# A two-layer float32 trunk on one core: norm weights and roots moved as whole rows, the first transfers and transposes re-ordered, the last residual added into the PSUM banks

## The chip, the core and the metric

The kernel runs on one core of one Trainium2 chip. TensorE (PE) multiplies matrices into the banks of PSUM; VectorE (DVE) and ScalarE (ACT) do the elementwise work between SBUF and PSUM; SyncE (SP), and ScalarE where the code says so, issue transfers (DMA). Each engine runs its own instructions in program order, and they wait for each other by semaphores. The metric is the device time of one execution in microseconds (us), lower is better.

## The reference

A causal decoder trunk on `x` of 1 x 1024 x 1024 float32, two layers. Each layer is a token mixer and a squared-ReLU MLP, each with an RMSNorm ahead and a residual add behind; a last RMSNorm gives the output.

```python
def reference(x, norm_mix_w, norm_mlp_w, final_norm_w, attn_w_in, ...):
    for i in range(2):
        h = rmsnorm(x, norm_mix_w[i])
        if i == 0: x = x + dilated_attention(h, attn_w_in[0], attn_w_out[0])
        else:      x = x + gla_mixer(h, gla_w_in[0], ...)
        h = rmsnorm(x, norm_mlp_w[i])
        a = relu(h @ mlp_w_up[i]);  x = x + (a * a) @ mlp_w_down[i]
    return rmsnorm(x, final_norm_w)
```

`rmsnorm(x, w)` is `x * rsqrt(mean(x*x) + 1e-5) * w` over the 1024 features. `dilated_attention` projects to queries, keys and values of three head groups, each with its own window and dilation; `gla_mixer` is gated linear attention in chunks of 64. The MLP is 1024 to 4096 to 1024.

## The kernel before, in words

All work is written out in program order, by hand, for every engine; there is no scheduler. A float32 product is made of three products of rounded parts: each operand is cut into a high part (`...h`, rounded by ScalarE) and a low part (`...l`, the rest, subtracted by VectorE), and high x high, high x low and low x high are summed in PSUM. On top of that the large products use a form with seven half-size products in place of eight, so that also sums of blocks (`s1` to `s4`) are cut.

**The start.** The first product is the values projection (`vals`), made from the raw `x`, with the norm's weights multiplied in as `x` is turned, and the norm's root (one number for each token) multiplied in as results leave PSUM. A constant tile `warm` is multiplied three times at L1533, for which nothing waits. Meanwhile SP issues the transfers in this order: the columns from 512 on of the first 128 tokens of `x`, the identity, the same columns of the next 128 tokens, the norm weights (`wcol`, one column of 128 weights per block of 128 features, read element by element at L1542), the first two weight blocks `raw` of 512 KB, the other columns of `x`, two more blocks `kept`, then the rest of `x`. A semaphore pool of eight serves SP's transfers in rotation.

`first_turn` (L334) transposes 256 tokens x 512 features of `x` through PSUM in eight 128 x 128 pieces, in two banks of four. `first_high` (L340, ScalarE) rounds each bank times `wcol` into `a12h` (later `a11h`). `first_low` (L346 and L348, VectorE) writes the unrounded float32 copy `a` from the bank and then subtracts. `rounded` (L1038, ScalarE) and `remain` (L1044, VectorE) cut a weight block into `dh` and `dl`. Then `product(n, blocks)` (L1060) multiplies: products 0 and 1 with `a12`, 2 and 3 with `a11`, each first for the token blocks [0, 1], then for [2, 3]; product 4 is the first with a sum (`s1`). With its third argument it takes the parts in the order high-high, high-low, low-high for all blocks, so that the low weights are wanted last.

`turn(p)` (transposes L318, copies by ScalarE L321) does the same for the next 256 tokens each; `cut` rounds (ScalarE L356) and subtracts (VectorE L358) the halves; `squares` sums the squares of `x` (ScalarE L1570, VectorE L1567); `roots(half)` makes the roots (`rstd_of`, L213 to L222) and stores them column-wise, element by element, to `rscr` in DRAM (L1575), from where the attention reads them as a row far later (L1678). `total`, `sums` and `sum1` to `sum4` make sums of blocks and of results on VectorE and ScalarE (L1014, L1142, L1146, L362). From step 8 on a loop takes one product after the other.

**The end.** The last MLP's down projection (`Down`) keeps the two halves of the result in PSUM (`pA`, `pB`) and the running residual in `xs`. Its steps 0 to 55 are again products of 24 matmuls. After step 53 the last two, 54 and 55, run for one block of 128 tokens at a time, and as each block is done, `add` puts the bank `pB` and the residual together into `xs` (VectorE, L1928), `half_out` sums its squares (ScalarE, L2006; the other half was done before), `root` and `small` make the norm's factor (L2027 to L2035), and `upper` (ScalarE, L2040) and `lower` (VectorE, L2045) scale the two halves and store them. One block's factor is finished while the next block multiplies.

Of the kernel before, what the change touches and what calls it, by code (L numbers as in the profile page):

```python
# [41 lines left out]
def hybrid_trunk(ctx, tc, x, norm_mix, norm_mlp, norm_fin, a_in, a_out, g_in, g_up, g_b, g_nw,  # L42
# [16 lines left out]
    def t2(shape, dt, name):  # L59
        return wk.tile(shape, dt, name=name, tag="t2", bufs=8)  # L60
# [4 lines left out]
    def sm(shape, name):  # L65
        return wk.tile(shape, F32, name=name, tag="sm", bufs=19)
# [215 lines left out]
    class Halves:  # L282
# [40 lines left out]
        def first_turn(self, c):  # L323

            name = ("a11", "a12")[c]
            self.a[0, c] = self.one("a", F32)
            self.up.h[name] = Split(self.one(name + "h", F32R), self.one(name + "l", F32R))
            self.ps = getattr(self, "ps", {})
            for kp in range(2):
                ps = self.ps[c, kp] = bank("pT").rearrange("p (k t) -> p k t", k=2)  # L330
                for k in range(2):
                    for i in range(2):
                        col = 512 * c + 256 * kp + 128 * k
                        pe.transpose(ps[:, k, 128 * i:128 * i + 128], self.xn[0][i][:, col:col + 128], ident)  # L334
# [7 lines left out]
        def first_low(self, c, kp):  # L342
            ps, s, a = self.ps.pop((c, kp)), self.up.h[("a11", "a12")[c]], self.a[0, c]
            for k in range(2):
                n = 2 * kp + k
                dve.tensor_scalar(a[0][:, n, :256], ps[:, k, :], self.wcol[:, 4 * c + n:4 * c + n + 1], None, op0=OP.mult)  # L346
            sl = slice(2 * kp, 2 * kp + 2)
            dve.tensor_tensor(s.lo[0][:, sl, :256], a[0][:, sl, :256], s.hi[0][:, sl, :256].bitcast(F32), op=OP.subtract)  # L348
# [1183 lines left out]
    for n in range(3):  # L1532
        pe.matmul(ps, warm[:, :128], warm, start=True, stop=True)  # L1533
    wcol = sm([P, KT], "wcol")
    x0 = [[k4([P, D], F32, "x0") for _ in range(2)] for _ in range(NB // 2)]

    def load_x0(p, i, sl=slice(0, D)):
        sp.dma_start(x0[p][i][:, sl], x[0, 256 * p + 128 * i:256 * p + 128 * i + 128, sl])
    load_x0(0, 0, slice(512, D))
    sp.dma_start(ident, ident_d)  # L1540
    load_x0(0, 1, slice(512, D))
    sp.dma_start(wcol, norm_mix[0].rearrange("(k p) -> p k", p=P))  # L1542
    vals.load(0)
# [13 lines left out]
    hs.wcol = wcol  # L1557
# [14 lines left out]
    def roots(half):  # L1572

        y = vals.roots[half] = rstd_of(sums[half], 4, 1.0 / D)
        sp.dma_start(rscr[512 * half:512 * half + 512].rearrange("(t p) -> p t", p=P), y)  # L1575

    hs.first_turn(1)
    hs.first_high(1, 0)
    hs.first_low(1, 0)
    vals.rounded(0)  # L1580
    hs.first_high(1, 1)
    vals.remain(0)
    hs.first_low(1, 1)
    vals.rounded(1)
# [9 lines left out]
    vals.rounded(3)  # L1594
    vals.remain(3)
# [11 lines left out]
    vals.product(0, [2, 3])  # L1607
    vals.sums(2)
    vals.product(1, [2, 3])
    vals.sums(4)  # L1610
    squares(1)
    hs.turn(2)
    hs.sum1(0)
    hs.cut("s1", 0)
    vals.product(2, [2, 3])
    vals.total(4)
    hs.turn(3)
    vals.sums(3)
    vals.rounded(4)
# [45 lines left out]
    for n in range(8, vals.STEPS):  # L1665
        if n == 9:
            for c in range(2):
                hs.cut("a22", c)
        if n >= 10:
            ahead.step()  # L1670
# [176 lines left out]
    class Down:  # L1847
# [153 lines left out]
        def half_out(self, t, n):  # L2001
            ss, o = self.fin[t]
            sl = slice(512 * n, 512 * n + 512)
            r = self.rows(4 + t)[:, sl]
# [6 lines left out]
        def run_end(self):  # L2011
# [31 lines left out]
            def lower(t, y):  # L2043
                o = self.fin.pop(t)[1][:, :512]
                dve.scalar_tensor_tensor(o, self.rows(4 + t)[:, :512], y, self.wbc[:, :512], op0=OP.mult, op1=OP.mult)  # L2045
                sp.dma_start(out[0, 512 + 128 * t:640 + 128 * t, :512], o)

            for t in range(4):
# [5 lines left out]
                self.add("B", 1, t, 0)  # L2054
# [506 lines left out]
```

## Time and profile before

| | us |
|---|---|
| median of 3 runs (lowest, highest) | 2576.76 (2575.3, 2578.85) |
| profiled execution, its own time | 2576.74 |
| its span | 2574.6 |
| PE busy | 2560.6 |
| DVE busy | 1865.7 |
| ACT busy | 1281.0 |

The granted TensorE clock of the profiled execution is 0.999. In the rows of the profile, `128x512 f32` is partitions x elements and type of what is written, `x4` a number of like instructions shown as one row, and `[1.46 <-ACT dh L1038]` the idle time of the engine ahead of the instruction and what ended it. PEld is TensorE's loading of the stationary operand, SPq and ACTq are issues of transfers. Matmuls are pipelined: a duration of 0.39 stands for one matmul by itself, the pace is the distance of the starts.

### The profile page before, as it was taken

Reading aid. Unit: us, or ns where it says so; the run is one execution under the profiler, and the core shown is the slowest. Engines: PE = TensorE matmul, PEld = TensorE weight load, DVE = VectorE, ACT = ScalarE, POOL = GpSimd, SP = SyncE. Lnnn points to the kernel's source line nnn. Section 1 sums busy time; section 2 is a strip of 40 time slices with the busy share of each in tenths; the row PEclk is TensorE's granted clock in tenths of the full one; section 3 lists DMA queues with packets and bytes.
Section 4 is the critical chain, followed back from the end, with each engine's and each line's share of the span. In section 5 each row is a group of like instructions: output and inputs, shape, how many; then the busy total and the mean of one; then the engine's idle time right before and its main releaser. Section 6 shows DMA issues by size and latency. Waiting matters only on the chain.

```text
span 2574.6 us, 34634 instructions
## 1 busy us (share of the span) xinstructions
PE 2560.6 (99%) x12582; PEld 2119.2 (82%) x12582; DVE 1865.7 (72%) x2990; ACT 1281.0 (50%) x2326; POOL 20.2 (1%) x24
## 2 busy tenths in 40 slices
PE   9999999999999999999999999999999999999998
PEld 7888888888888888888888888888888888888887
DVE  7766888888888766788668795787666666566666
ACT  6443445555555445666534453554335555453344
POOL 0000000000000000000000000110000000000000
PEclk9999999999999999999999999999999999999999
DMA  6886465656566747799788865777545644495543
GB/s 170 269 274 199 107 162 142 161 148 153 153 156 175 240 172 253 267 334 338 267 322 290 280 220 196 262 248 283 174 162 199 236 158 139 147 348 199 187 148 128
DMA packets 359196, 544.86 MB, mean 212 GB/s; under 512 B 26640, under 2 KB 182672, under 8 KB 359024
## 3 DMA queue, kind: packets, MB, share of 16 engines
q1 hardware_dynamic: 358880, 542.38, 64.8%
q8 instruction: 99, 1.62, 0.3%
q14 instruction: 73, 0.60, 0.1%
q10 hardware_dynamic: 144, 0.26, 0.0%
HBM read 339.45 MB, written 177.93 MB: 201 GB/s over the span
## 4 chain that ended last, share of the span: by engine, by line
PE 67%; DVE 2%; DMA 1%; ACT 1%; issue 1%; SPq 0%; DVEq 0%; ACTq 0%
PE pB L1922 14%; PE pX L848 11%; PE pA L1922 10%; PE pV L848 8%; PE pY L848 4%; PE pZ L848 4%; PE pB L1060 3%; PE pA L1060 3%; PE pd L196 2%; PE pd L198 2%; PE pd L197 2%; PE pT L259 1%; PE pO L2384 1%; PE pO L2382 0%; PE pU L2365 0%
## 5 line engine op out<-in xcount | busy, mean ns | idle before, releaser
L1922 PE MATMUL pB<-dh 128*128 128x512 f32 x512 | 199.2, 389 | 0.0
L1922 PE MATMUL pB<-dl,dh 128*128 128x512 f32 x512 | 199.2, 389 | 0.0
L1922 PE MATMUL pB<-dh,dl 128*128 128x512 f32 x512 | 199.2, 389 | 0.0
L205 DVE TENSOR_TENSOR dl<-sin,dh 128x1024 fp32r<-128x1024 f32 x112 | 136.6, 1220 | 61.7 <-ACT dh L202 58.9
L848 PE MATMUL pV<-s4h,wd 128*128 128x512 f32 x480 | 161.5, 398 | 0.4 <-DVE qk L2118 0.4
L202 ACT ACTIVATE dh<-sin 128x1024 fp32r<-128x1024 f32 x112 | 117.8, 1052 | 78.6 <-PE pB L1922 29.9
L1922 PE MATMUL pA<-dh 128*128 128x512 f32 x384 | 149.6, 390 | 0.0
L1922 PE MATMUL pA<-dh,dl 128*128 128x512 f32 x384 | 149.4, 389 | 0.0
L1922 PE MATMUL pA<-dl,dh 128*128 128x512 f32 x384 | 149.4, 389 | 0.0
L853 ACT ACTIVATE e<-pX 128x512 f32<-128x512 f32 x108 | 64.4, 596 | 154.3 <-PE pX L848 154.2
L202 ACT ACTIVATE dh<-kept 128x1024 fp32r<-128x1024 f32 x64 | 67.8, 1060 | 146.4 <-DVE kept L1887 102.0
L786 DVE TENSOR_TENSOR wbl<-t,wbh 128x1024 fp32r<-128x1024 f32 x48 | 58.8, 1226 | 78.8 <-ACT wbh L785 78.8
L1922 PEld LDWEIGHTS pB<-dl,dh 128*128 128x128 f32 x512 | 96.1, 188 | 20.1
L1922 PEld LDWEIGHTS pB<-dh,dl 128*128 128x128 f32 x512 | 96.1, 188 | 19.9
L1922 PEld LDWEIGHTS pB<-dh 128*128 128x128 f32 x512 | 96.1, 188 | 19.9
L848 PEld LDWEIGHTS pV<-s4h,wd 128*128 128x128 f32 x480 | 90.1, 188 | 20.3 <-DVE qk L2118 0.8
L1210 ACT ACTIVATE pt<-pt,orow 128x256 f32<-128x256 f32 (+1 forms) x128 | 59.8, 468 | 92.7 <-DVE orow L1208 89.4
L848 PE MATMUL pX<-s3h,wgh 128*128 128x512 f32 x240 | 96.8, 403 | 0.0
L848 PE MATMUL pX<-s2h,wbh 128*128 128x512 f32 x240 | 95.9, 400 | 0.1
L848 PE MATMUL pV<-s1h,wbh 128*128 128x512 f32 x240 | 95.6, 398 | 0.0
L848 PE MATMUL pY<-a12h,wah 128*128 128x512 f32 x240 | 95.3, 397 | 0.0
L848 PE MATMUL pX<-a11h,wah 128*128 128x512 f32 x240 | 95.0, 396 | 0.0
(369 smaller groups left out, 7232.1 us busy)
## 6 DMA issues: line engine op xcount, KB each, us to landing
sin<-acts SPq DMA_DIRECT2D x112, 512.0 KB, 4.3
acts<-s SPq DMA_DIRECT2D x64, 512.0 KB, 3.5
raw<-in_mlp_w_down_dram SPq DMA_DIRECT2D x64, 512.0 KB, 5.1
raw<-in_attn_w_in_dram SPq DMA_DIRECT2D x96, 256.0 KB, 4.4
cw<-c SPq DMA_DIRECT2D x192, 128.0 KB, 2.3
raw<-in_mlp_w_up_dram SPq DMA_DIRECT2D x48, 512.0 KB, 6.1
acts<-c SPq DMA_DIRECT2D x64, 256.0 KB, 3.3
kept<-in_mlp_w_down_dram SPq DMA_DIRECT2D x32, 512.0 KB, 7.3
```

What stands on the lines that cost most here:

```text
L196: pe.matmul(ps, sh, mh, start=start, stop=False)
L197: pe.matmul(ps, sh, ml, start=False, stop=False)
L198: pe.matmul(ps, sl, mh, start=False, stop=stop)
L202: act.activation(hi, src, AF.Copy)
L205: dve.tensor_tensor(lo, src, hi.bitcast(F32), op=OP.subtract)
L259: pe.transpose(ps[e][:, 64 * n:64 * n + 64], src[k, :], ident[k, k], tile_position=(64 * e, 0))
L786: self.remain(lambda: dve.tensor_tensor(lo, src, hi.bitcast(F32), op=OP.subtract))
L848: pe.matmul(st[b], u[:, k, :], v, start=first and k + n == 0, stop=k == 3 and n == 2, skip_group_check=True)
L853: act.activation(e, self.st[p]["X"], AF.Copy)
L1060: pe.matmul(self.acc[s][t], parts[k][v == 2][:, 128 * t:128 * t + 128], (th, tl)[v == 1][:, k, :], start=fresh and m + k + v == 0, stop=m ...
L1210: act.activation(pt[:, i, :128 * n], pt[:, i, :128 * n], AF.Exp, scale=-1.0, bias=m, accum_out=self.row[:, r, HD:HD + 1])
L1922: pe.matmul(self.acc[s][t], a[:, k, c], b[:, k, :], start=fresh and m + k + v == 0, stop=m == 7 and k == 1 and v == 2, skip_group_check=True)
```

## The change

Line numbers move by 6 at the start and by some 30 at the end. What it does:

- The constant tile is multiplied once with 512 and once with 256 columns (L1539) in place of three times with 512.
- The norm weights come as 8 rows of 128 (`wrow`), are transposed on TensorE (L1592) and copied to `wcol` by ScalarE (L1593).
- The second piece of `x` is issued on ScalarE's queue (L1543) in place of SP's, and the first weight block comes as two loads of 256 KB (L1551). Its rounding is shared: the first half by VectorE (L1597), the second by ScalarE (L1599).
- `first_turn` can do one bank of four transposes at a time, and the first copies stand between the two.
- `first_low` subtracts straight from the bank (one fused operation for each 128 x 256, L347); the float32 copy `a` is made by ScalarE (`first_keep`, L354), eight instructions of 128 x 256.
- `roots` no longer stores; `spread(half)` transposes the roots (L1586), copies the 4 x 128 result (ScalarE, L1588) and stores rows. It stands behind `turn(3)` for the first half and in step 14 for the second.
- Product 0 for the blocks [2, 3] is cut in two, with `turn(2)`'s halves between; `turn(3)` stands ahead of product 2 for [2, 3]; `squares(1)` and the sums around it move with them.
- At the end, four additions of the residual into the four banks `pB` (L2079) stand ahead of products 54 and 55, which go on adding to these banks; `half_out` and `lower` read the bank.

ScalarE's program at the start shows several of these at once. Before (numbers behind the names are buffers; `raw` and `kept` are weight blocks, `pT` a bank of transposes):

```order
L963 ACT_TABLE_LOAD
L340 ACTIVATE a12h_248<-pT_250,wcol_215 128x256 x2
L1038 ACTIVATE dh_265<-raw_228 128x1024
L340 ACTIVATE a12h_248<-pT_255,wcol_215 128x256 x2
L1038 ACTIVATE dh_274<-raw_230 128x1024
L340 ACTIVATE a11h_295<-pT_297,wcol_215 128x256 x2
L1038 ACTIVATE dh_312<-kept_234 128x1024
```

and with the change:

```order
L969 ACT_TABLE_LOAD
L1543 DMA x0_215<-in_x_dram 128x512
L1593 ACTIVATE wcol_247<-pT_248 128x8
L341 ACTIVATE a12h_252<-pT_254,wcol_247 128x256 x2
L1599 ACTIVATE dh_259<-raw_227 128x512
L341 ACTIVATE a12h_252<-pT_264,wcol_247 128x256 x2
L1044 ACTIVATE dh_275<-raw_230 128x1024
L354 ACTIVATE a_251<-pT_254,wcol_247 128x256 x2
L354 ACTIVATE a_251<-pT_264,wcol_247 128x256 x2
L341 ACTIVATE a11h_302<-pT_304,wcol_247 128x256 x2
L1044 ACTIVATE dh_318<-kept_234 128x1024
```

A transfer stands ahead of the first copy, the first rounding is half as long, and the copies at L354 stand between the second block's rounding and the next turned half.

VectorE's program at the end, before, from the last block's add on (`xs` is the residual, `fin` the output rows, `v`, `t`, `y` the root's small numbers):

```order
L1928 TENSOR_TENSOR xs_20421<-pB_21814,xs_20421 128x512
L2045 SCALAR_TENSOR_TENSOR fin_22007<-xs_20421,y_22114,wbc_21452 128x512
L2028 TENSOR_SCALAR v_22141<-ss_22012 128x1
L2033 SCALAR_TENSOR_TENSOR t_22143<-y_22142,v_22141 128x1
L2034 TENSOR_SCALAR t_22143<-t_22143 128x1
```

and with the change, from the adds on, which now stand ahead of the first block's root:

```order
L2079 TENSOR_TENSOR pB_21828<-pB_21828,xs_20364 128x512
L2079 TENSOR_TENSOR pB_21829<-pB_21829,xs_20364 128x512
L2079 TENSOR_TENSOR pB_21830<-pB_21830,xs_20438 128x512
L2079 TENSOR_TENSOR pB_21831<-pB_21831,xs_20438 128x512
L2058 TENSOR_SCALAR v_22077<-ss_21978 128x1
L2063 SCALAR_TENSOR_TENSOR t_22079<-y_22078,v_22077 128x1
```

The adds are no longer between a block's last matmul and its square sum; all four come together.

The diff, cut to its core:

```diff
@@ -320,16 +320,17 @@
                 for k in range(2):
                     act.activation(dst[:, k, :], ps[:, k, :], AF.Copy, scale=self.wcol[:, 2 * kp + k:2 * kp + k + 1])
 
-        def first_turn(self, c):
+        def first_turn(self, c, kps=(0, 1)):
 
             name = ("a11", "a12")[c]
-            self.a[0, c] = self.one("a", F32)
-            self.up.h[name] = Split(self.one(name + "h", F32R), self.one(name + "l", F32R))
+            if kps[0] == 0:
+                self.a[0, c] = self.one("a", F32)
+                self.up.h[name] = Split(self.one(name + "h", F32R), self.one(name + "l", F32R))
             self.ps = getattr(self, "ps", {})
-            for kp in range(2):
+            for kp in kps:
                 ps = self.ps[c, kp] = bank("pT").rearrange("p (k t) -> p k t", k=2)
-                for k in range(2):
-                    for i in range(2):
+                for i in range(2):
+                    for k in range(2):
                         col = 512 * c + 256 * kp + 128 * k
                         pe.transpose(ps[:, k, 128 * i:128 * i + 128], self.xn[0][i][:, col:col + 128], ident)
 
@@ -340,12 +341,17 @@
                 act.activation(s.hi[0][:, n, :256], ps[:, k, :], AF.Copy, scale=self.wcol[:, 4 * c + n:4 * c + n + 1])
 
         def first_low(self, c, kp):
-            ps, s, a = self.ps.pop((c, kp)), self.up.h[("a11", "a12")[c]], self.a[0, c]
+            ps, s = self.ps[c, kp], self.up.h[("a11", "a12")[c]]
             for k in range(2):
                 n = 2 * kp + k
-                dve.tensor_scalar(a[0][:, n, :256], ps[:, k, :], self.wcol[:, 4 * c + n:4 * c + n + 1], None, op0=OP.mult)
-            sl = slice(2 * kp, 2 * kp + 2)
-            dve.tensor_tensor(s.lo[0][:, sl, :256], a[0][:, sl, :256], s.hi[0][:, sl, :256].bitcast(F32), op=OP.subtract)
+                dve.scalar_tensor_tensor(s.lo[0][:, n, :256], ps[:, k, :], self.wcol[:, 4 * c + n:4 * c + n + 1],
+                                         s.hi[0][:, n, :256].bitcast(F32), op0=OP.mult, op1=OP.subtract)
+
+        def first_keep(self, c, kp):
+            ps, a = self.ps.pop((c, kp)), self.a[0, c]
+            for k in range(2):
+                n = 2 * kp + k
+                act.activation(a[0][:, n, :256], ps[:, k, :], AF.Copy, scale=self.wcol[:, 4 * c + n:4 * c + n + 1])
 
         def split(self, name, src, c, hi, lo):
             h = self.up.h
@@ -1529,18 +1535,20 @@
     warm = t2([P, 512], F32, "warm")
     dve.memset(warm, 0.0)
     ps = bank("pw")
-    for n in range(3):
-        pe.matmul(ps, warm[:, :128], warm, start=True, stop=True)
-    wcol = sm([P, KT], "wcol")
+    for n in (512, 256):
+        pe.matmul(ps[:, :n], warm[:, :128], warm[:, :n], start=True, stop=True)
     x0 = [[k4([P, D], F32, "x0") for _ in range(2)] for _ in range(NB // 2)]
 
-    def load_x0(p, i, sl=slice(0, D)):
-        sp.dma_start(x0[p][i][:, sl], x[0, 256 * p + 128 * i:256 * p + 128 * i + 128, sl])
+    def load_x0(p, i, sl=slice(0, D), eng=sp):
+        eng.dma_start(x0[p][i][:, sl], x[0, 256 * p + 128 * i:256 * p + 128 * i + 128, sl])
+    wrow = t2([P, 512], F32, "wrow")
     load_x0(0, 0, slice(512, D))
+    load_x0(0, 1, slice(512, D), act)
     sp.dma_start(ident, ident_d)
-    load_x0(0, 1, slice(512, D))
-    sp.dma_start(wcol, norm_mix[0].rearrange("(k p) -> p k", p=P))
-    vals.load(0)
+    sp.dma_start(wrow[:KT, :P], norm_mix[0].rearrange("(k p) -> k p", p=P))
+    t = vals.raw[0] = k4([P, 2, 512], F32, "raw")
+    for k in range(2):
+        sp.dma_start(t[:, k, :], a_in[512 + 128 * k:640 + 128 * k, vals.first[0]:vals.first[0] + 512])
     vals.load(1)
     for i in range(2):
         load_x0(0, i, slice(0, 512))
@@ -1554,7 +1562,7 @@
         k = slice(64 * e, 64 * e + 64)
         sp.dma_start(masks[k, 256:320], msk[k, 128 + 64 * e:192 + 64 * e])
     hs = Halves(None, None, vals, None)
-    hs.wcol = wcol
+    wcol = hs.wcol = sm([P, KT], "wcol")
     hs.xn = dict(enumerate(x0))
 
     sums = {}
@@ -1572,16 +1580,31 @@
     def roots(half):
 
         y = vals.roots[half] = rstd_of(sums[half], 4, 1.0 / D)
-        sp.dma_start(rscr[512 * half:512 * half + 512].rearrange("(t p) -> p t", p=P), y)
-
-    hs.first_turn(1)
+
+    def spread(half):
+        ps = bank("pT")
+        pe.transpose(ps[:4, :P], vals.roots[half], ident)
+        t = t2([P, 512], F32, "rrow")
+        act.activation(t[:4, :P], ps[:4, :P], AF.Copy)
+        sp.dma_start(rscr[512 * half:512 * half + 512].rearrange("(t p) -> t p", p=P), t[:4, :P])
+
+    ps = bank("pT")
+    pe.transpose(ps[:, :KT], wrow[:KT, :P], ident[:KT, :KT])
+    act.activation(wcol, ps[:, :KT], AF.Copy)
+    hs.first_turn(1, (0,))
+    th = k4([P, 2, 512], F32R, "dh")
+    vals.cut[0] = th, vals.raw.pop(0)
+    dve.tensor_copy(th[:, 0, :], vals.cut[0][1][:, 0, :])
     hs.first_high(1, 0)
+    act.activation(th[:, 1, :], vals.cut[0][1][:, 1, :], AF.Copy)
+    hs.first_turn(1, (1,))
     hs.first_low(1, 0)
-    vals.rounded(0)
+    vals.remain(0)
     hs.first_high(1, 1)
-    vals.remain(0)
+    vals.rounded(1)
+    hs.first_keep(1, 0)
     hs.first_low(1, 1)
-    vals.rounded(1)
+    hs.first_keep(1, 1)
     vals.remain(1)
     vals.product(0, [0, 1], True)
     hs.first_turn(0)
@@ -1592,6 +1615,8 @@
     vals.remain(2)
     hs.first_low(0, 1)
     vals.rounded(3)
+    hs.first_keep(0, 0)
+    hs.first_keep(0, 1)
     vals.remain(3)
     vals.product(1, [0, 1], True)
     vals.product(2, [0, 1], True)
@@ -1604,19 +1629,22 @@
     vals.load(5)
     hs.cut("a11", 1)
     roots(0)
-    vals.product(0, [2, 3])
+    vals.product(0, [2], True)
+    hs.turn(2, (0, 2))
+    vals.product(0, [3], True)
+    hs.turn(2, (1, 3))
     vals.sums(2)
+    hs.sum1(0)
     vals.product(1, [2, 3])
+    hs.cut("s1", 0)
     vals.sums(4)
+    hs.turn(3)
+    spread(0)
+    vals.total(4)
+    vals.rounded(4)
+    vals.sums(3)
     squares(1)
-    hs.turn(2)
-    hs.sum1(0)
-    hs.cut("s1", 0)
     vals.product(2, [2, 3])
-    vals.total(4)
-    hs.turn(3)
-    vals.sums(3)
-    vals.rounded(4)
     vals.total(5)
     vals.remain(4)
     vals.rounded(5)
@@ -1666,6 +1694,8 @@
         if n == 9:
             for c in range(2):
                 hs.cut("a22", c)
+        if n == 14:
+            spread(1)
         if n >= 10:
             ahead.step()
         if n == vals.STEPS - 4:
@@ -2001,7 +2031,7 @@
         def half_out(self, t, n):
             ss, o = self.fin[t]
             sl = slice(512 * n, 512 * n + 512)
-            r = self.rows(4 + t)[:, sl]
+            r = self.rows(4 + t)[:, sl] if n else self.acc["B"][t]
             junk = t2([P, 512], F32, "junk")
             act.activation(junk, r, AF.Square, accum_out=ss[:, n:n + 1])
             if n:
@@ -2042,16 +2072,17 @@
 
             def lower(t, y):
                 o = self.fin.pop(t)[1][:, :512]
-                dve.scalar_tensor_tensor(o, self.rows(4 + t)[:, :512], y, self.wbc[:, :512], op0=OP.mult, op1=OP.mult)
+                dve.scalar_tensor_tensor(o, self.acc["B"][t], y, self.wbc[:, :512], op0=OP.mult, op1=OP.mult)
                 sp.dma_start(out[0, 512 + 128 * t:640 + 128 * t, :512], o)
 
+            for t in range(4):
+                dve.tensor_tensor(self.acc["B"][t], self.acc["B"][t], self.rows(4 + t)[:, :512], op=OP.add)
             for t in range(4):
                 self.product(54, [t])
                 self.product(55, [t])
                 if t:
                     y = small(t - 1)
                     upper(t - 1, y)
-                self.add("B", 1, t, 0)
                 if t:
                     lower(t - 1, y)
                 self.half_out(t, 0)
```

## The prediction

> **What bounds the kernel now.** I read the page first, then the timelines of both ends, the transfers by the moment of their issue, and the middle only where the ends run into it. The page says that the profiled execution is TensorE from end to end:
>
> ```profile
> PE 2560.6 (99%) x12582; PEld 2119.2 (82%) x12582; DVE 1865.7 (72%) x2990; ACT 1281.0 (50%) x2326; POOL 20.2 (1%) x24
> ```
>
> The span is 2574.6, the execution's own time 2576.74, so 2.14 us lie around the span; the median of the runs is 2576.76, the same number. Only 14.0 us of the span have no matmul in them, so an edit at the ends can win a few microseconds at most. 0.2%, about what a measurement of this kernel tells from no change, is 5.15 us.
>
> **The start.** TensorE counts as busy there while it only warms up on zeros, or crawls:
>
> ```profile
> 0.73 1.28 ACT L963 ACT_TABLE_LOAD   x1 [0.73 <-PEq L2550]
> 1.48 5.14 PE L1533 MATMUL pw<-warm 128*128 128x512 f32 x6 [1.48 <-DVE warm L1530]
> 6.46 1.04 PE L334 MATMUL pT<-ident,x 128*128 128x128 f32 x8
> 7.84 1.06 ACT L1038 ACTIVATE dh<-raw 128x1024 fp32r<-128x1024 f32 x1
> 8.95 1.19 PE L1060 MATMUL pB<-dh,a12h 128*128 128x512 f32 x4 [1.46 <-ACT dh L1038]
> 11.82 1.04 PE L334 MATMUL pT<-ident,x 128*128 128x128 f32 x8
> 19.83 1.17 PE L1060 MATMUL pA<-dh,a11h 128*128 128x512 f32 x4
> ```
>
> The columns are start, duration, engine, line, operation. The first transposes stand at 6.46, product 0 from 8.95 to 11.82, product 3 at 19.83. What they wait for are transfers:
>
> ```profile
> 1.65 0.42 SPq L1538 DMA_DIRECT2D x<-in_x_dram  x1
> 2.59 1.57 SPq L1004 DMA_DIRECT2D raw<-in_attn_w_in_dram  x2
> ...
> x<-in_x_dram SPq DMA_DIRECT2D x1, 256.0 KB, 3.5
> wcol<-in_norm_mix_w_dram SPq DMA_DIRECT2D x1, 4.0 KB, 4.0
> raw<-in_attn_w_in_dram SPq DMA_DIRECT2D x1, 512.0 KB, 5.2
> raw<-in_attn_w_in_dram SPq DMA_DIRECT2D x1, 512.0 KB, 6.1
> x<-in_x_dram SPq DMA_DIRECT2D x1, 256.0 KB, 5.8
> ...
> 3.50:4.00 0.50, 0.50 (x2) 0.19 (x1) 0.00 (x0) 0.00 (x0) 0.00 (x0) 1.00 0.96 291
> 4.00:4.50 0.50, 0.50 (x2) 0.29 (x1) 0.00 (x0) 0.00 (x0) 0.00 (x0) 1.00 0.60 61
> 4.50:5.00 0.50, 0.50 (x1) 0.04 (x1) 0.00 (x0) 0.00 (x0) 0.00 (x0) 1.00 0.44 31
> ```
>
> The last number of an issue is microseconds to landing; the last three of a window are granted clock, share of the DMA engines and GB/s. Issued at 1.65, the x half lands at 5.2; the norm weights, issued between it and 2.59, land some 4.0 later, about 6.1; the two weight blocks (2.59, and half of 1.57 later) at 7.8 and 9.5. While the 1024 single elements of the norm weights are in flight the engines move 61 and 31 GB/s instead of 291. The two windows lost (230 + 260) x 0.5 = 245 KB, 0.84 us at 291 GB/s; I take 0.9.
>
> **The middle.** Product 4, the first after the shared start, waits for ScalarE and then VectorE:
>
> ```profile
> 33.71 3.16 ACT L321 ACTIVATE a<-pT,wcol 128x256 f32<-128x256 f32 x8
> 34.60 1.38 PE L318 MATMUL pT<-ident,x 128*128 128x128 f32 x8 [0.49 <-ACT a L321]
> 39.00 1.23 DVE L1044 TENSOR_TENSOR dl<-kept,dh 128x1024 fp32r<-128x1024 f32 x1 [2.31 <-ACT dh L1038]
> 39.02 1.20 PE L1060 MATMUL pB<-dh,s1h 128*128 128x512 f32 x4 [0.28 <-ACT dh L1038]
> 55.98 0.19 PEld L1060 LDWEIGHTS pA<-dl,s2h 128*128 128x128 f32 x1 [0.35 <-DVE dl L1044]
> 40.00:44.00 4.00, 4.00 (x19) 3.29 (x19) 4.00 (x7) 1.24 (x2) 0.00 (x0) 1.00 0.31 112
> ```
>
> From 40 to 44 VectorE has no free time (4.00 of 4.00, the number behind PEld's), and at 55.98 TensorE is held up by it. What the start wins reaches the end of the kernel only as far as VectorE's chain, which begins at 39.00 with `dl`, also comes earlier.
>
> **Step 1, transfers.** With the norm weights as 8 whole rows, the 0.9 us come back. The first weights, now two loads of 256 KB, land at 7.8 - 0.9 = 6.9, the second block at 9.5 - 0.9 = 8.6. The x half on ACT's queue is issued behind the table load, 0.73 + 1.28 = 2.01, instead of at 1.65. Its price there is in no row; bounds are the first load's and those of the loads queued behind the weights (5.8): 0.74 + 2.9 = 3.6 as the earliest landing, 7.8 as the latest. I take the row of the same transfer, 3.5, so 5.5:
>
> ```profile
> 0.74 0.39 SPq L1538 DMA_DIRECT2D x<-in_x_dram  x1
> x<-in_x_dram SPq DMA_DIRECT2D x1, 256.0 KB, 2.9
> ```
>
> What is queued behind the issue on ACT is its first copy, which needs the data anyway. Up to about 5.9 the landing costs nothing, since product 0 then waits for the weights; each us later costs one.
>
> SP's queue has one issue less (the x half) and one more (the weights' second load), about 0.4 us each, so what stands behind them is issued as before.
>
> **Step 2, from the landing to product 0.** Transposes at 5.5, the wcol transpose and its copy ahead of them hidden, a pair of copies (0.84 in the row, 0.74 to ScalarE's next start at 7.84), rounding of the first half by VectorE as the weights land (6.9 plus 0.53, half of the 1.06 of the whole block, to 0.69, the 128x512 row), the second by ScalarE; product 0's `dl` part waits for one subtraction of 1.23 (the `dl` row at 39.00). Before, product 0's twelve matmuls took 8.95 to 11.82, 0.24 each; four of them behind a `dl` ready at about 8.8 then end near 9.8 instead of 11.82. The second block's weights (8.6 + 1.06 + 1.23 = 10.9 for the remainder, needed by product 1's last four) allow product 1 2.0 us earlier too.
>
> ```profile
> 7.10 0.84 ACT L340 ACTIVATE a12h<-pT,wcol 128x256 fp32r<-128x256 f32 x2 [5.08 <-PE pT L334]
> 7.97 0.88 DVE L346 TENSOR_SCALAR a<-pT,wcol 128x256 f32<-128x256 f32 x2 [6.54 <-ACT a12h L340]
> 8.88 0.69 DVE L348 TENSOR_TENSOR a12l<-a,a12h 128x512 fp32r<-128x512 f32 x1
> 15.80 1.07 ACT L1570 ACTIVATE junk<-x 128x1024 bf16<-128x1024 f32 x1
> 20.41 1.06 ACT L356 ACTIVATE a12h<-a 128x1024 fp32r<-128x1024 f32 x1
> 30.17 0.19 PEld L1060 LDWEIGHTS pA<-dh,a11h 128*128 128x128 f32 x1 [0.41 <-ACT a L321]
> ```
>
> **Step 3, work that moves to ScalarE.** VectorE's pair plus subtraction (0.88 + 0.69 per half) becomes two fused operations from PSUM. No row shows that form on 128x256: it lies between 0.35, half of the 128x512 subtraction, and 0.79, a copy of the pair plus half of that subtraction (0.44 + 0.35); I take 0.44, the row that reads the same bank. This frees 4 x 0.69 = 2.8 us of VectorE. In return ScalarE makes the eight f32 copies, 0.40 each by the eight at L321 (3.16), so 3.2 us between 8.6 and 19. ScalarE's work from the second block on, each 0.1 under its row since rows overlap as the pair's does: roundings 3 x 0.96, pairs 2 x 0.74, eight copies 3.2, two squares 2.1, four copies 1.6 and the cut of 0.96 end at 8.6 + 12.2 = 20.8; before, the same cut ends at 21.5. ScalarE has no idle time left in this stretch, and wins only 0.7 us of the 2.0. Where product 0's second half waits for that cut and its VectorE remainder, TensorE loses some 0.8 us, and again 0.7 in product 2, at the copies of its last transposes. The spreading of the transposes between products wins part of it back: the stalls at 30.17 and 34.60 (0.41 and 0.49, and 0.5 of the slow pace behind them) go, 1.4 in all. Done by rows for each engine up to product 4 this comes to 36.75 instead of 39.02: 2.3 us.
>
> **Step 4, into the VectorE stretch.** `dl` of product 4's block stands at about 36.1 in the same working, 2.9 earlier. So VectorE's chain gains more than TensorE's, and of the small stalls behind it (0.35 at 55.98) part goes. I take 2.4 us for the start, bounds 2.3 and 2.9. The moved squares and `total` are the same instructions; the second roots' three loose operations are hidden under 24 matmuls per product.
>
> **Step 5, the roots.** The column-wise store of 512 elements becomes a 4x128 transpose, a small copy and a row store, twice. Its landing frees nothing early: `rscr` is read at 224.7. TensorE pays three small transposes of about 0.1 each, two of them outside the idle start, and ScalarE the two copies: 0.1 us at most stays, taken whole.
>
> **Step 6, the tail.**
>
> ```profile
> 2559.43 0.69 DVE L1928 TENSOR_TENSOR xs<-pB,xs 128x512 f32<-128x512 f32 x1 [8.58 <-PE pB L1922]
> 2567.17 0.39 PE L1922 MATMUL pB<-dh,dl 128*128 128x512 f32 x1
> 2567.59 0.69 DVE L1928 TENSOR_TENSOR xs<-pB,xs 128x512 f32<-128x512 f32 x1
> 2567.61 0.72 ACT L2040 ACTIVATE fin<-fin,y 128x512 f32<-128x512 f32 x1 [0.73 <-PE pB L1922]
> 2568.32 0.63 ACT L2006 ACTIVATE junk<-xs 128x512 f32<-128x512 f32 x1
> ```
>
> The last add (2567.59, 0.69, handoff 0.04) stands between the last matmul and the square at 2568.32. Without it the square starts as the bank is done, 2567.6; the scaling ahead of it on ScalarE (2567.61) comes 0.7 earlier with its own chain. That is -0.7 us. The four adds move into VectorE's 8.58 us of idle time. Each waits for its own bank's last matmul of product 53; the first bank is done 9 matmuls, 2.0 us, before product 54 touches it, so an add of 0.69 has 1.35 us to spare. Were this cover gone, one add would stand in front of product 54 and take the 0.7 back. The square and the last scaling read the bank where they read a row before; ScalarE's copies out of banks above (0.40 for 256) speak for no loss beyond 0.2, which I leave to the range.
>
> **The sum**: 2576.74 - 2.4 - 0.7 + 0.1 = 2573.7.
>
> **Rivals.** (1) All stalls of the start go: the stalls of step 3 after product 0 (0.8 + 0.7) do not come since the copies are shorter than I think, and VectorE's chain follows. Then 2573.7 - 1.5, and another 0.9 for the short waits like that at 55.98, of which this needs two or three: 2571.3. For it: ScalarE's rows are busy spans with overlaps. Against: VectorE's 4.00 of 4.00. Chance 0.15.
>
> (2) The pace of TensorE. Weight loads take 0.34 us while it warms up and 0.14 for the same shape later:
>
> ```profile
> L1533 PEld LDWEIGHTS pw<-warm x6: 288/338/338, 1.5 to 5.1; 128*128 128x128 f32 x6
> L334 PEld LDWEIGHTS pT<-ident,x x16: 139/141/231, 5.9 to 12.5; 128*128 128x128 f32 x16
> ```
>
> The quick pace came 4.4 to 5.0 us after the first matmul. The changed warm-up is half as long and ends near 1.48 + 3 x 0.86 = 4.05 (half of the row's 5.14); then TensorE idles till 5.5. If the pace must be earned anew from there, product 0 runs at up to 0.338/0.141 = 2.4 times its time, which adds some 2 us to its first eight matmuls; half of it hides behind the wait for `dl`, 1.0 stays: 2574.7, 0.13. The granted clock reads 1.00 throughout, so the page's clock row cannot decide it. The Trainium skill (TensorE: Matmul & The Clock Gate, "Part 1: The HAM clock gate") has full clock only after a busy window of about 3.4 us; the trace's durations agree (0.338 before 5.1, 0.141 after 5.9), its clock column does not.
>
> (3) Slower: the x half on ACT's queue lands late, because it is issued after the table load and stands behind the weight loads. From 5.9 each us costs one; the gain of 3.0 is gone, and no more is won, at a landing of about 9.0, which is 7.0 us after the issue. The row of the 512 KB block of x, queued deeper, shows 9.3:
>
> ```profile
> x<-in_x_dram SPq DMA_DIRECT2D x6, 512.0 KB, 9.3
> ```
>
> At 9.3 it lands at 11.3, 5.4 past 5.9: 2573.7 + 5.4 = 2579.1. Against it: only 320 KB, x and the identity, are issued ahead of it. 0.05.
>
> (4) Given back in the VectorE stretch: `dl` comes no earlier than TensorE's own gain of 0.6 there, because the eight copies delay ScalarE's roundings ahead of it: 2576.74 - 0.6 - 0.7 + 0.1 = 2575.5, 0.09.
>
> (5) The x half takes the 5.8 of the x load that is issued among the weight loads, and lands at 7.8: the 1.9 past 5.9 go, for 2575.6. For it, its weight-load neighbours are issued within 1 us; against, the 3.5 and 2.9 of the issues at 1.65 and 0.74, of which the one had two transfers before it. 0.10. The Trainium skill (DMA: Bandwidth & Descriptors, "Issuing engines are not separate DMA queues") speaks for this one: transfers started by different engines run on the same 16 DMA engines and interleave, and another engine saves the issue alone; no row of this trace has two issuing engines at the start.
>
> **How the numbers follow.** Forecast 0.48, rivals in their order 0.15, 0.13, 0.05, 0.09, 0.10. The range takes in rival 1 with 0.7 of scatter below it, 2570.6, and ends 1.1 above rivals 4 and 5, at 2576.7; only rival 3 and the scatter of a median of three runs (2575.3 to 2578.85 before) lie outside, less than 2 in 10. Faster by over 0.2% is below 2571.6, which is most of rival 1 and little of the forecast: 0.15. Slower by over 0.2%, above 2581.9, needs rival 3 at its worst: 0.03. The rest, 0.82, is within 0.2%.
>
> **What would show it.** Transposes near 5.5 and not past 5.9 (step 1); product 0's first matmul near 7.2 and its end near 9.8 (step 2); ScalarE without idle time from 8.5 to 20 (step 3); the first `pB<-dh,s1h` near 36.7 (step 4); the square of the last block 0.0 instead of 0.7 after the last matmul (step 6), and the four adds done before product 54 needs them. A weight load of 0.34 in product 0 would speak for rival 2, transposes past 9 for rival 3, and product 4 early with longer VectorE waits behind it for rival 4.

## The result: slower by 27 us, spread over thousands of matmuls

The changed kernel takes 2604.02 us (median of 5, 2603.41 to 2606.11) against 2576.76 (2575.3 to 2578.85): a ratio of 1.0107, 95% interval 1.0092 to 1.0122. The forecast was 2573.7, with a range up to 2576.7. The profiled execution took 2605.88, its span is 2604.0.

The first lines of the page of the changed kernel:

```profile
span 2604.0 us, 34650 instructions
PE 2592.9 (100%) x12583; PEld 2119.9 (81%) x12583; DVE 1865.7 (72%) x2987; ACT 1283.4 (49%) x2337; POOL 20.3 (1%) x24
```

VectorE and ScalarE do what they did before (1865.7 and 1281.0 there), and TensorE has one instruction more. It is busy 32.3 us longer, and waits for less: 11.1 us of the span are without a matmul, 14.0 before. So the loss is no wait. It must lie in the pace, and a view that shows pace is the one by windows, because it counts. Before, then after; the columns are the window, its length, PE's busy time with the number of matmuls that run in it, granted clock, DMA share and GB/s:

```profile
100.00:200.00 100.00, 100.00 (x443) 1.00 0.83 287
1100.00:1200.00 100.00, 99.88 (x440) 1.00 0.98 334
1300.00:1400.00 100.00, 100.00 (x443) 1.00 0.82 292
2100.00:2200.00 100.00, 100.00 (x443) 1.00 0.45 153
2400.00:2500.00 100.00, 100.00 (x443) 1.00 0.49 158
```

```profile
100.00:200.00 100.00, 100.00 (x431) 1.00 0.79 271
1100.00:1200.00 100.00, 100.00 (x432) 1.00 0.97 334
1300.00:1400.00 100.00, 100.00 (x443) 1.00 0.85 303
2100.00:2200.00 100.00, 100.00 (x432) 1.00 0.45 152
2400.00:2500.00 100.00, 100.00 (x443) 1.00 0.54 174
```

In both kernels TensorE hardly rests in these windows (99.88 of 100 us at the least), and the granted clock is 1.00. In 100 us the kernel before runs 443 matmuls (440 in the window with the short rests); the changed one 431 or 432 in the values projection (100 to 200) and in the MLPs' up projections (1100 and 2100), and again 443 in the down projections (1300 and 2400). The starts themselves say the same more finely. The table has the mean distance of neighbouring starts (those of 215 to 245 ns), worked out from all starts of a line:

| product (line before, after) | matmuls | before, ns | after, ns |
|---|---|---|---|
| values, in the second layer also gates (L1060, L1066) | 1680 | 227.0 | 232.7 |
| up projections (L848, L854) | 5040 | 227.6 | 232.4 |
| down projections (L1922, L1952) | 2688 | 226.7 | 226.7 |

The line of the up projections, L848, also makes the attention's queries and keys (2016 of the 5040) and the keys of the second layer's mixer (336); the MLPs' own 2688 go from 226.8 and 226.7 in the two layers to 232.4 in both. Some 1650 and 4755 of the distances lie in the range: 1650 x 5.7 + 4755 x 4.8 ns = 9.4 + 22.8 = 32.2 us. That is more than the 29.4 us between the two profiled spans, so that the rest of the change must have won some of it back.

What do the slow lines have in common? Not the instructions, which are the same, but the addresses of their operands. The working tiles are cut from pools, one for each size of tile, which are laid out in the order in which they are first used (the addresses are those of the two built programs). Before, the small tiles' pool (19 tiles of 96 bytes per partition, 1824 bytes) is first used by `wcol`, ahead of `x0`, the first tile of the pool of 4 KB tiles. The change creates `wcol` later, behind `x0`, so the 4 KB pool moves down by 1824 bytes and the small pool goes behind it; the pool of 8 KB tiles stays:

| start, bytes in a partition | before | after |
|---|---|---|
| pool of 4 KB tiles (weights) | 21696 | 19872 |
| pool of 8 KB tiles (turned activations) | 124096 | 124096 |
| difference | 102400 = 400 x 256 | 104224 = 407 x 256 + 32 |

Most matmuls of the values and up lines take one operand from each pool; the down projections take both from the 4 KB pool, where nothing moves against each other. That was the theory to test. One group does not fit its simplest form, that each matmul goes by its own two operands: the low parts `s2l`, `s3l` and `s4l` lie in the 4 KB pool too, so the 720 matmuls at L854 and 240 at L1066 that use them have both operands there. They stand between matmuls that use both pools, and they are slower too: 231.0 and 233.4 ns from their start to the next (227.3 and 226.9 before).

### The profile page after: what moved, and what is told of

The parts are those of the page before. It is cut to its first block, busy times and chain, and to the rows that moved or that the text cites. A ratio compares the mean times of both kernels' runs of the same rounds, so it can differ in the third digit from the quotient of the medians.

```text
span 2604.0 us, 34650 instructions
## 1 busy us (share of the span) xinstructions
PE 2592.9 (100%) x12583; PEld 2119.9 (81%) x12583; DVE 1865.7 (72%) x2987; ACT 1283.4 (49%) x2337; POOL 20.3 (1%) x24
## 4 chain that ended last, share of the span: by engine, by line
PE 68%; DVE 2%; ACT 1%; DMA 1%; issue 0%; SPq 0%; DVEq 0%; ACTq 0%
PE pB L1952 13%; PE pX L854 12%; PE pA L1952 10%; PE pV L854 8%; PE pY L854 4%; PE pZ L854 4%; PE pB L1066 3%; PE pA L1066 3%; PE pd L196 2%; PE pd L197 2%; PE pd L198 2%; PE pT L259 1%; PE pO L2415 1%; PE pO L2413 0%; PE pU L2396 0%
## 5 line engine op out<-in xcount | busy, mean ns | idle before, releaser
L1952 PE MATMUL pB<-dl,dh 128*128 128x512 f32 x512 | 199.2, 389 | 0.0
L1952 PE MATMUL pB<-dh,dl 128*128 128x512 f32 x512 | 199.2, 389 | 0.0
L1952 PE MATMUL pB<-dh 128*128 128x512 f32 x512 | 199.2, 389 | 0.0
L854 PE MATMUL pV<-s4h,wd 128*128 128x512 f32 x480 | 163.0, 401 | 0.2 <-DVE qk L2149 0.2
L1952 PE MATMUL pA<-dh 128*128 128x512 f32 x384 | 149.6, 390 | 0.0
L1952 PE MATMUL pA<-dl,dh 128*128 128x512 f32 x384 | 149.4, 389 | 0.0
L1952 PE MATMUL pA<-dh,dl 128*128 128x512 f32 x384 | 149.4, 389 | 0.0
L1952 PEld LDWEIGHTS pB<-dh,dl 128*128 128x128 f32 x512 | 96.1, 188 | 20.1
L1952 PEld LDWEIGHTS pB<-dh 128*128 128x128 f32 x512 | 96.1, 188 | 19.9
L1952 PEld LDWEIGHTS pB<-dl,dh 128*128 128x128 f32 x512 | 96.1, 188 | 19.8
L854 PEld LDWEIGHTS pV<-s4h,wd 128*128 128x128 f32 x480 | 90.2, 188 | 21.5 <-DVE qk L2149 0.6
L854 PE MATMUL pX<-s3h,wgh 128*128 128x512 f32 x240 | 97.5, 406 | 0.0
L854 PE MATMUL pV<-s1h,wbh 128*128 128x512 f32 x240 | 96.7, 403 | 0.0
L854 PE MATMUL pY<-a12h,wah 128*128 128x512 f32 x240 | 96.4, 402 | 0.0
L854 PE MATMUL pX<-s2h,wbh 128*128 128x512 f32 x240 | 96.3, 401 | 0.0
L854 PE MATMUL pX<-a11h,wah 128*128 128x512 f32 x240 | 96.3, 401 | 0.0
```

Source lines behind the costliest of these rows:

```text
L854: pe.matmul(st[b], u[:, k, :], v, start=first and k + n == 0, stop=k == 3 and n == 2, skip_group_check=True)
L1952: pe.matmul(self.acc[s][t], a[:, k, c], b[:, k, :], start=fresh and m + k + v == 0, stop=m == 7 and k == 1 and v == 2, skip_group_check=True)
```

## Time at the two ends

The start of the changed kernel, from its timeline, then its TensorE windows and the first product with a sum:

```profile
0.73 1.28 ACT L969 ACT_TABLE_LOAD   x1 [0.73 <-PEq L2581]
0.76 0.39 ACTq L1543 DMA_DIRECT2D x<-in_x_dram  x1
4.77 1.09 PE L335 MATMUL pT<-ident,x 128*128 128x128 f32 x8
7.39 2.00 PE L1066 MATMUL pB<-dh,a12h 128*128 128x512 f32 x4 [1.53 <-DVE dh L1597]
11.96 1.04 PE L335 MATMUL pT<-ident,x 128*128 128x128 f32 x8
...
6.00:7.00 1.00, 0.00 (x0) 1.00 0.93 340
8.00:9.00 1.00, 1.00 (x3) 0.50 1.01 307
...
L1066 PE MATMUL pB<-dh,s1h x16: 395/396/396, 38.4 to 47.5; 128*128 128x512 f32 x16
```

The transposes stand at 4.77 (6.46 before), product 0 at 7.39 (8.95). But TensorE had nothing to do from 6 to 7 us, and from 7.8 to 11.2 us the granted clock is 0.50: the first four matmuls take 2.00 us instead of 1.19 (part of this is a wait for the second half of the weights; without the half clock they take 1.56, as a run below shows), and the next transposes come at 11.96, later than the 11.82 of before. Product 4 starts at 38.4 instead of 39.02.

The end:

```profile
2584.59 2.74 DVE L2079 TENSOR_TENSOR pB<-pB,xs 128x512 f32<-128x512 f32 x4 [3.81 <-PE pB L1952]
2597.08 0.39 PE L1952 MATMUL pB<-dh,dl 128*128 128x512 f32 x1
2597.51 0.60 ACT L2036 ACTIVATE junk<-pB 128x512 f32<-128x512 f32 x1
2600.18 0.38 ACTq L2071 DMA_DIRECT2D out_dram<-fin  x1
```

From the last matmul's start to its block's square it is 0.43 us (1.15 before), to the last issue 3.10 (3.86 before). The four adds are done at 2587.3 and no matmul waits for them.

## Experiments: is it the place of the tiles?

**Addresses of before, all else changed.**

```diff
+    wcol = sm([P, KT], "wcol")
     x0 = [[k4([P, D], F32, "x0") for _ in range(2)] for _ in range(NB // 2)]
...
-    wcol = hs.wcol = sm([P, KT], "wcol")
+    hs.wcol = wcol
```

> The changed kernel with one line moved: the small tile wcol is allocated ahead of the x0 tiles again, as in the kernel before, so every tile of the large working pools gets back its address of before. Theory A (placement): the matmuls' distance of 232.5 ns comes with their two operands lying at different places within 64 bytes; with the addresses of before it is 226.7 everywhere, the 33 us of longer distances (1658 x 5.7 ns in the values projection, 4883 x 4.7 ns in the MLPs' up projections, under 1 us elsewhere) go, and the time is about 2571 us. Rival B (clock): the half-clock window that the trace of after shows at 7.8 to 11.2 us leaves TensorE slower for long stretches; the time stays at 2604. Rival C (PSUM): the three added bank allocations shift which banks the products write; the time stays at 2604.

Measured: 2573.53 us (2572.43 to 2576.78), a ratio to before of 0.9988 (0.9979 to 0.9997), so 30.5 us less than the changed kernel, for a line that moves no instruction. About 2571 had been expected. Its windows:

```profile
100.00:200.00 100.00, 100.00 (x443) 1.00 0.80 279
1100.00:1200.00 100.00, 99.91 (x441) 1.00 0.97 331
2100.00:2200.00 100.00, 100.00 (x443) 1.00 0.43 146
```

The distances are those of before (227.0, 227.6, 226.7 ns). Like matmuls of this run and of the changed kernel draw apart by 30.7 us inside the stretches of the values and up lines and by less than 0.1 us in the down projections; their spans differ by 31.8. Rivals B and C fall: the three added bank allocations are still there, and so is the short warm-up. This version is faster than the changed kernel and, by some 3 us, than the kernel before.

**Addresses of after, all else as before.**

```diff
-    wcol = sm([P, KT], "wcol")
     x0 = [[k4([P, D], F32, "x0") for _ in range(2)] for _ in range(NB // 2)]
+    wcol = sm([P, KT], "wcol")
```

> The kernel before with the two allocations of wcol and x0 exchanged and nothing else: no instruction moves, only addresses. A: the distances of after's L854 and L1066 appear here too, 2576.8 + 33 = about 2610 us. B and C: no change, 2576.8 us.

Measured: 2608.43 us, ratio 1.0122 (1.0109 to 1.0136), 31.3 us more than the kernel before run beside it (2577.11). The distances are after's: 232.7, 232.5 and 226.7 ns. So the exchange of two lines is enough for the whole loss, in both directions. (It moves the small tiles' pool as well; the unused tiles of the next runs do not.)

**How fine is the grain?** An unused tile between the two pools sets their difference; nothing else changes. With 64 bytes:

```diff
     x0 = [[k4([P, D], F32, "x0") for _ in range(2)] for _ in range(NB // 2)]
+    wk.tile([P, 16], F32, name="pad", tag="pad", bufs=1)
```

> The kernel before with an unused tile of 64 bytes per partition between the pool of 4 KB tiles and the pool of 8 KB tiles, so that the two operands of the values and up projections lie 64 bytes apart modulo 4096 (0 in the kernel before; in after the offset is 32 modulo 64). A with a grain of 64 bytes: no change, 2576.8 us. A with a wider grain (any offset counts): about 2610 us. B and C: 2576.8 us.

and with 128, 256 and 512 bytes (`[P, 32]`, `[P, 64]`, `[P, 128]`):

> As the run with 64 bytes between the two pools, with 128 bytes. Read from the distance of the matmuls in the up projections (L848: 226.7 ns with offset 0 for most, 230.9 with 64, 232.5 with an offset of 32 modulo 64). Grain of 128 bytes: 226.7 and about 2576.8 us. Wider grain: 230 ns or more and 2595 to 2610 us. If the offset may also help: under 226.7 ns, under 2570 us.

> The same with 256 bytes. Grain of 256 bytes or less: 226.7 ns and about 2576.8 us. Wider grain: 230 ns or more and 2595 to 2610 us. A rank by distance (the further from 0 the better or worse) would show between the values for 64 and 128.

> The same with 512 bytes, which is the step by which the operands' own slices already lie apart. If only the offset modulo 512 counts: 226.7 ns and 2576.8 us. If the two pools have to lie a multiple of 4096 apart: 230 ns or more, 2595 to 2610 us.

**Both pools moved alike.**

```diff
+    cst.tile([P, 8], F32, name="pad")
     warm = t2([P, 512], F32, "warm")
```

> The kernel before with an unused tile of 32 bytes ahead of all working pools: both operands of every large matmul lie at 32 modulo 64. A (their relation counts): no change, 2576.8 us. Rival D (each operand must itself lie at a multiple of 64 bytes): all of some 10000 large matmuls at 232.5 ns, the down projections at L1922 too, about 2576.8 + 57 = 2634 us.

All of them together (128, 256 and 512 bytes are single runs; distances from all starts as above, under the same names):

| 4 KB pool against 8 KB pool, modulo 256 | kernel | us | values, ns | up, ns | down, ns |
|---|---|---|---|---|---|
| 0 | before | 2576.76 | 227.0 | 227.6 | 226.7 |
| 0, both at +32 | both moved by 32 | 2576.83 | 227.0 | 227.6 | 226.7 |
| 0 | 256 between | 2576.69 | 227.0 | 227.6 | 226.7 |
| 0 | 512 between | 2575.7 | 227.0 | 227.6 | 226.7 |
| 32 | exchanged lines | 2608.43 | 232.7 | 232.5 | 226.7 |
| 64 | 64 between | 2601.82 | 233.3 | 230.9 | 226.7 |
| 128 | 128 between | 2603.04 | 232.8 | 231.2 | 226.7 |

The windows of the two sides of the border, 128 bytes and then 256:

```profile
1100.00:1200.00 100.00, 100.00 (x433) 1.00 0.98 339
1300.00:1400.00 100.00, 100.00 (x443) 1.00 0.85 300
```

```profile
1100.00:1200.00 100.00, 99.89 (x441) 1.00 0.97 333
1300.00:1400.00 100.00, 100.00 (x443) 1.00 0.84 292
```

Rival D falls: two operands that both lie 32 bytes off keep the pace. What counts is how the two pools of operands lie to each other, and of the differences tried it costs nothing at multiples of 256 bytes (0, 256, 512) and 25 to 31 us at 32, 64 and 128. My first guess of a grain, 64 bytes, was wrong. No offset was better than 0. Two things stay open. Because the matmuls with `s2l`, `s3l` and `s4l` slow down with the rest, a matmul's own pair is not the whole relation; an operand and that of a neighbouring matmul may count as well, and no run separates the two. And why the pace depends on the places at all is not shown: no run took the read of the streamed operand and the load of the next stationary one apart.

## Experiments: what the rest of the change did

With the addresses put back, the prediction's own terms can be read. The kernel of the first experiment:

```profile
4.71 1.97 PE L335 MATMUL pT<-ident,x 128*128 128x128 f32 x8
7.41 1.56 PE L1066 MATMUL pB<-dh,a12h 128*128 128x512 f32 x4 [0.74 <-DVE dh L1598]
10.64 1.03 PE L335 MATMUL pT<-ident,x 128*128 128x128 f32 x8
19.76 1.06 ACT L362 ACTIVATE a12h<-a 128x1024 fp32r<-128x1024 f32 x1
22.13 0.30 PEld L1066 LDWEIGHTS pB<-dh,a12l 128*128 128x128 f32 x2 [0.46 <-DVE a12l L364]
31.34 0.19 PEld L1066 LDWEIGHTS pA<-dh,a11h 128*128 128x128 f32 x1 [0.57 <-ACT a L321]
36.44 1.22 DVE L1050 TENSOR_TENSOR dl<-kept,dh 128x1024 fp32r<-128x1024 f32 x1
36.72 0.87 PEld L1066 LDWEIGHTS pB<-dh,s1h 128*128 128x128 f32 x4
36.95 1.07 PE L1066 MATMUL pB<-dh,s1h 128*128 128x512 f32 x4
53.40 0.19 PEld L1066 LDWEIGHTS pA<-dl,s2h 128*128 128x128 f32 x1 [0.17 <-DVE dl L1050]
...
2565.32 0.39 PE L1953 MATMUL pB<-dh,dl 128*128 128x512 f32 x1
2568.41 0.39 ACTq L2072 DMA_DIRECT2D out_dram<-fin  x1
```

Product 4's weights are loaded from 36.72 and its first matmul starts at 36.95 (both 39.02 before). Against like matmuls of the kernel before, the work stands some 2.55 us earlier at 62 to 94 us, 2.40 from 96 to beyond 246, as little as 1.1 at the end of the attention, 2.3 where the first MLP begins (953), 1.9 from 1093 on, and 1.85 in the second layer's MLP. The end wins 3.86 - (2568.41 - 2565.32) = 0.77.

**The end alone**, on the kernel before:

```diff
+            for t in range(4):
+                dve.tensor_tensor(self.acc["B"][t], self.acc["B"][t], self.rows(4 + t)[:, :512], op=OP.add)
             for t in range(4):
                 self.product(54, [t])
                 self.product(55, [t])
...
-                self.add("B", 1, t, 0)
```

(with `half_out` and `lower` reading the bank, as in the change)

> The kernel before with the change's last part alone: the four residual adds ahead of products 54 and 55, the square and the last scaling read the bank. As predicted for this part: the time from the last matmul's start to the last issue falls from 3.86 us by 0.7, the matmuls before are untouched, 2576.0 us. If one of the adds stood in front of product 54: the 0.7 us come back as a wait of TensorE, 2576.8 us.

Measured: 2576.68 us, ratio 0.9996 (0.9987 to 1.0004): 0.7 us is too small for this comparison, and the time decides nothing. The profile does:

```profile
2555.34 2.74 DVE L2049 TENSOR_TENSOR pB<-pB,xs 128x512 f32<-128x512 f32 x4 [3.82 <-PE pB L1922]
2567.83 0.39 PE L1922 MATMUL pB<-dh,dl 128*128 128x512 f32 x1
2568.25 0.60 ACT L2006 ACTIVATE junk<-pB 128x512 f32<-128x512 f32 x1
2570.92 0.39 ACTq L2041 DMA_DIRECT2D out_dram<-fin  x1
```

From the last matmul to the last issue 3.09 us instead of 3.86, with the adds in VectorE's idle time. In this execution a longer wait for the first `dh`, which the edit does not touch (2.75 us against 1.46), took the gain back: the last matmul starts 0.66 later than before.

**The warm-up.** The half clock in the changed kernel's trace asked for the long warm-up again, on the kernel of the first experiment:

```diff
-    for n in (512, 256):
+    for n in (512, 512, 512):
```

> The changed kernel with the addresses of before and the long warm-up of before (three times 512 columns, which end near 6.6 us instead of 4.4). If the short warm-up is harmless: the transposes start 1.9 us later (6.6 instead of 4.7), product 0 starts about 0.9 later (the pair of copies after the transposes, 6.6 + 0.6 + 0.7 + 0.3 = 8.3 against 7.4), so about 2574.4 against 2573.5 us. If the short warm-up costs (a half-clock window in product 0, seen at 7.8 to 11.2 us in after's trace, in part of the executions): up to 1.4 us less in those, so 2573 us or below in the median. Either lies near what the comparison can tell; the profile's start is read beside it.

Measured: 2573.54 us (2571.31 to 2574.84) against 2573.53 (2572.43 to 2576.78) with the short one: no difference that can be told. Its start:

```profile
1.48 4.52 PE L1539 MATMUL pw<-warm 128*128 128x512 f32 x6 [1.48 <-DVE warm L1536]
6.09 1.09 PE L335 MATMUL pT<-ident,x 128*128 128x128 f32 x8
7.37 0.73 PE L1066 MATMUL pB<-dh,a12h 128*128 128x512 f32 x2 [0.19 <-ACT a12h L341]
36.94 0.87 PEld L1066 LDWEIGHTS pB<-dh,s1h 128*128 128x128 f32 x4
```

The quick pace comes during the warm-up (the trace's first record of the clock, 1.00, begins at 4.9 us in this execution; where there is no record the windows print 1.00 too), the transposes later, and product 0 no later than with the short warm-up (7.37 and 7.41). The late transposes cost nothing here because product 0 of the short warm-up waited for something else: the rounded first weights (0.74 us), where this one waits for ScalarE's copies (0.19).

**ScalarE's added copies.** Four of the eight f32 copies back on VectorE (`True` makes `first_keep` use VectorE's `tensor_scalar`), first with the short warm-up:

```diff
-    hs.first_keep(0, 0)
-    hs.first_keep(0, 1)
     vals.remain(3)
+    hs.first_keep(0, 0, True)
+    hs.first_keep(0, 1, True)
```

> The changed kernel with the addresses of before, and four of ScalarE's eight float32 copies of the first 256 tokens (those of a11) back on VectorE, behind its remainder of the fourth weight block. If ScalarE's extra copies bound the stretch from 14 to 23 us, as the prediction's step on the work that moves to ScalarE says: the a12 cut comes up to 1.6 us earlier (19.76 to about 18.2), the 0.46 us wait for a12l at 22.13 goes, and product 4 starts 0.5 to 1.5 us earlier than 36.72, 2572 to 2573 us. If VectorE has no room: its own squares and remainders are late by 1.8 us, and product 4 does not start earlier.

Measured: 2574.21 us, ratio 0.9987 (0.9978 to 0.9996). Its profiled execution cannot be compared at the start, as TensorE kept the slow pace through all of product 0:

```profile
7.29 2.31 PE L1070 MATMUL pB<-dh,a12h 128*128 128x512 f32 x4 [0.56 <-DVE dh L1602]
11.10 1.91 PE L1070 MATMUL pB<-dl,a12h 128*128 128x512 f32 x4
12.80 1.50 PE L335 MATMUL pT<-ident,x 128*128 128x128 f32 x8
```

So again with the long warm-up:

> The changed kernel with the addresses of before, the long warm-up and the four copies of a11 on VectorE. In the trace of the same kernel with the short warm-up TensorE kept its slow pace until 13.7 us, so its start could not be compared; with the long one it can, with the run that had the long warm-up alone (product 4 at 36.94 us, 2573.54 us). If ScalarE's extra copies bound the stretch: product 4 at 36.4 or earlier, 2572.5 to 2573 us. If not: product 4 at 36.9 or later, 2573.5 us.

Measured: 2573.39 us (2571.88 to 2576.15), and

```profile
12.05 1.17 PE L1070 MATMUL pB<-dh,a12h 128*128 128x512 f32 x4
19.84 1.06 ACT L366 ACTIVATE a12h<-a 128x1024 fp32r<-128x1024 f32 x1
37.02 0.87 PEld L1070 LDWEIGHTS pB<-dh,s1h 128*128 128x128 f32 x4
```

By the letter of the expectation, product 4 after 36.9 and the time speak against the copies as a bound. But product 1 began 0.43 us later here (12.05 against 11.62 in the run with the long warm-up alone), so from there on the stretch is 0.35 shorter, and the wait for `a12l` (0.48 with the long warm-up alone) is gone. The copies cost something like that in this one pair of executions, not the 1.6 us I expected: the a12 cut stayed at 19.84, since the copies ahead of it then wait for TensorE's transposes.

## Why the prediction was wrong, and where it was right

The step that failed is the first: "Only 14.0 us of the span have no matmul in them, so an edit at the ends can win a few microseconds at most". It took the distance of 12,000 matmuls as given, as did the costing part by part: the new place of the line that makes `wcol` moves no instruction, so it was priced at nothing and not even named. It cost 30.5 us (31.3 by the reverse experiment). None of the five rivals had it; the slower one (a late x half) did not happen.

With the addresses of before, what the prediction did price comes out near its sum, 2573.53 against 2573.7. To some extent this is luck: by the trace the start is worth 1.85 us at the end of the run, not 2.4, and the executions of this version scatter from 2572.43 to 2576.78. Its terms, read there:

- Step 1 had a wrong row of mechanism: the x half is issued on ScalarE's queue at 0.76, during the table load, not behind it at 2.01. It landed 3.5 later, so the transposes came at 4.7 instead of 5.5; rivals 3 and 5 went with it. The first weights' two loads landed near 6.8 and 7.5 (6.9 predicted for both).
- Step 2 was too large: product 0 started at 7.41 (about 7.2 was written, but 6.9 plus the 0.53 of the rounding is 7.4) and ended near 10.6, not 9.8, because its second half of weights came late. Product 1 was 1.2 us earlier than before, not 2.0.
- Step 3: the a12 cut ended at 20.8 as worked out. The waits behind it were smaller than the 0.8 and 0.7 taken: 0.46 at 22.13 and 0.57 at 31.34. Together with product 1's smaller gain this put product 4's first matmul at 36.95, against 36.75. The terms that the step shows (2.0 - 0.8 - 0.7 + 1.4) make 1.9, not the 2.3 it states; the trace has 2.1.
- Step 4: `dl` at 36.44, 2.6 us earlier, not 2.9; the later wait fell from 0.35 to 0.17; 2.40 us were left at 200 us, as forecast. The further loss, to 1.9 us from 1093 us on, was not foreseen.
- Step 5's 0.1 us was not read by itself.
- Step 6 held: 0.77 for 0.7, and the adds wait for nobody but their banks.
- Rival 2, the pace of TensorE, is real but comes and goes with the execution: half clock from 7.8 to 11.2 us in the changed kernel's trace, slow matmuls through all of product 0 in one experiment's, none after 7 us in the first experiment's. In the one execution it put the next transposes 12.80 - 10.64 = 2.2 us back, more than the 1.0 given. Its time is inside the scatter of the runs. The clock row that "cannot decide it" had no record to show: in the trace of the kernel before the first one begins at 6.14 us.

## What to carry to other kernels

An edit that moves the first use of a pool can move other pools: compare the tiles' addresses of the two programs, not only their instructions. In this kernel the large matmuls kept their pace where the pools of their operands lay a multiple of 256 bytes apart. When TensorE is 99% busy or more in both profiles and yet the time differs, count matmuls by window; equal busy time hides another pace. A few microseconds saved at a start are small beside 2% on thousands of matmuls.

## What the runs showed that I had not expected

- The mean distance of 128x128 by 512 matmuls went from 227.0 and 227.6 ns to 231 to 233 ns when the pools of the two operands lay 32, 64 or 128 bytes apart modulo 256, at a granted clock of 1.00, and stayed at 227.0 and 227.6 for 0, 256 and 512. Matmuls between these slowed down too, though both of their operands came from one pool.
- A transfer issue of ScalarE ran at 0.76 us, while its table load took 0.73 to 2.01.
- The clock at the start differs between executions: after the short warm-up the first record of 1.00 begins at 6.8 us in one, at 4.4 with a half-clock stretch from 7.8 to 11.2 in another, and in a third only at 13.7.
